# Causal mask added to the diagonal attention scores on TensorE, unmasked copies shared between ScalarE and VectorE

## The chip, the cores and the metric

The kernel runs on one core of a Trainium2 chip. The metric is the device time of one execution in microseconds (us), the median of the runs; less is better. Five engines work side by side, each through its own queue in order: TensorE (PE, with its weight loads shown apart as PEld), VectorE (DVE), ScalarE (ACT), GpSimd (POOL) and SyncE (SP), which issues most DMAs.

## The reference, cut to what matters

The program is one layer of a hybrid decoder for a prompt of 2048 tokens and for a small sample group. The change touches one of its four branches, the stick-breaking attention of the prompt: 8 heads of 64, strictly causal.

```python
def sb_block(q, k, v, bias, q_pos, k_pos):
    z = (jnp.einsum('nqhd,nkhd->nhqk', q, k).astype(jnp.float32) * (SB_HEAD_DIM ** -0.5)
         + bias.astype(jnp.float32)[None, :, None, None])
    mask = (k_pos[None, :] < q_pos[:, None])[None, None]
    log_beta = jax.nn.log_sigmoid(z)
    log_1m = jnp.where(mask, jax.nn.log_sigmoid(-z), 0.0)
    rc = lax.cumsum(log_1m, axis=3, reverse=True)
    a = jnp.exp(jnp.where(mask, log_beta + rc - log_1m, -jnp.inf))
    return jnp.einsum('nqhk,nkhd->nqhd', a.astype(v.dtype), v)
```

The kernel works without logarithms: with beta = sigmoid(z) and gamma = sigmoid(-z), the weight of key k is beta(k) times the product of gamma over all later visible keys. A key at or after its query must count as beta 0 and gamma 1.

## The kernel before, in words

The program has three stages that follow each other on TensorE: the input projections, with the sample group's attention over its cache beside them (to about 1476 us); the prompt's stick-breaking attention (`sb_prompt`, to about 1950 us), with bits of side work; and the output projection.

The attention runs over 4 head pairs (`hp`), and in each over 4 blocks of 512 queries (`qb`). A block goes through its chunks of 512 keys (`kc`) from the diagonal one (`kc == qb`, called `dg`) down to 0: 16 diagonal steps and 24 others. A step has 4 score pairs (two heads `hh`, times two pairs of 128-query tiles, `q2` = 0 and 2) and 8 turned tiles (4 rows `r` of 128 keys, times two heads):

- `score`: TensorE forms S (line L1267, two matmuls `x` for each of two query tiles `j`); ScalarE turns S into gamma (`gam`, L1271) and beta (`be`, L1272); VectorE runs the product from the right as a scan (`E`, L1337 on the diagonal, L1340 elsewhere); GpSimd multiplies beta by it (L1349). On the diagonal the width w is 256 for `q2` = 0 and 512 for `q2` = 2.
- `turn`: six score steps later TensorE transposes the weights of 128 keys into a PSUM tile `AT` (L1360; two buffers), and a copy takes them to SBUF as `at` (four buffers). On the diagonal the copy is VectorE's and multiplies by the triangle `tri`, which drops keys that are not before the query (L1364); elsewhere it is ScalarE's plain copy (L1366).
- `values`: two steps later again TensorE adds `at` times V into `av` (L1376). At the end of a block VectorE multiplies `av` by the gate (`sbo`, L1381), and `av` has one buffer.

The scan of a diagonal tile multiplies by unmasked gammas and takes the maximum with `ZM`, a PSUM tile that holds 1 from the query's own key on, so that the product starts anew there.

The order on TensorE is the order in which the code is written. On the other engines a scheduler orders the instructions when the program is built. The first two score pairs (`sb_early`, tile `Se`) are formed during the projections. Side work on the output weights, the convolution branch and the end of the sample group is let in by costs that `sb_prompt` yields with each step.

Of the kernel before, what the change touches and what calls it, by code (L numbers as in the profile page):

```python
# [8 lines left out]
F32 = mybir.dt.float32  # L9
F32R = mybir.dt.float32r  # L10
# [3 lines left out]
ALU = mybir.AluOpType  # L14
# [4 lines left out]
P = 128  # L19
# [43 lines left out]
KT = 2  # L63
WR = 2


# [22 lines left out]
def kernel(  # L89
# [69 lines left out]
    ident = con.tile([P, P], F32, name="ident")  # L159
# [1077 lines left out]
    def sb_loader(sbr):  # L1237

        KT, V = {}, {}

        def load(hp, qb):
# [19 lines left out]

        return load, values

    def sb_scores(S, h, q2, w, Q, kt):
        for j in range(2):
            for x in range(2):
                pe.matmul(S[:, j, :w], lhsT=Q[:, x, P * (q2 + j) : P * (q2 + j + 1)], rhs=kt[:, :w], start=x == 0,  # L1267
                          stop=x == 1)

    def sb_gates(S, h, w, ga, be):  # L1270
        act.activation(out=ga, in_=S[:, :, :w], func=AF.Sigmoid, bias=nbias_bc[:, h : h + 1], scale=-1.0)  # L1271
        act.activation(out=be, in_=S[:, :, :w], func=AF.Sigmoid, bias=bias_bc[:, h : h + 1])  # L1272

    def sb_early(load, blk, sbr, bps, early):

        room = sbr.tile([P, 16, P], F32, tag="V", name="early", bufs=2).rearrange("p (n j b) c -> p n j (b c)", n=4, j=2)
        for n in range(2):
            blk[0, n] = load(0, n)
        for _ in range(3):
            yield  # L1280
        for hh in range(2):
            S = bps.tile([P, 512], F32, tag="AT", name=f"Se{hh}", bufs=2).rearrange("p (j k) -> p j k", j=2)
            Q, KT, _ = blk[0, 0]
            sb_scores(S, hh, 0, 2 * P, Q[hh], KT[0, hh, 0])
# [4 lines left out]
    def sb_prompt(load, loaded, sb, bps, ops, zmp, early, values_of, flags, newest):  # L1289

# [63 lines left out]
        def turn(hp, qb, kc, r, hh):  # L1354
# [7 lines left out]
            c = slice(P * q0, 512)  # L1362
            if dg:
                dve.tensor_tensor(out=at[:, c], in0=ap_[:, c], in1=tri[:, : 512 - P * q0], op=ALU.mult)  # L1364
            else:
                act.copy(at[:, c], ap_[:, c])  # L1366
            ats[hp, qb, kc, r, hh] = at
# [513 lines left out]
    S = {}  # L1881
# [23 lines left out]
    for cost in main():  # L1905
        tasks.step()
        due += rate * cost
        while sample is not None and due >= 1.0:
            due -= 1.0
            try:  # L1910
# [5 lines left out]
                sbr = bx.enter_context(tc.tile_pool(name="sbr", bufs=1, side="right", reuse_waits="tile"))  # L1916
                load, values_of = sb_loader(sbr)
                bps = bx.enter_context(tc.tile_pool(name="bps", bufs=1, space=PSUM, side="right", reuse_waits="tile"))
                starts = sb_early(load, blk, sbr, bps, early)
                next(starts)  # L1920
# [86 lines left out]
    due, steps = 0.0, 0  # L2007
    for cost in sb_prompt(load, blk, sb, bps, ops, zmp, early, values_of, flags, newest):
        steps += 1
# [164 lines left out]
```

## Time and profile before

| | |
|---|---|
| runs of the kernel before | 2357.12, 2351.18, 2350.86 us; median 2351.18 |
| profiled execution, first to last instruction | 2357.7 us |
| mean granted TensorE clock | 0.994 |
| PE busy over the whole span | 2270.5 us, 96% |
| window 1485 to 1950 us (attention) | PE 441.1, DVE 391.0, ACT 400.1, POOL 371.1 of 465 us |

The page and the answers give busy times by engine and line, idle times with what ended them, and the order in time. A busy PE is not a PE at its peak, since the ends of its pipelined matmuls are modelled: what one matmul costs its successors is the distance between starts, not its length. For the profiled execution the span is the only time known; it lies 6.5 us over the median of the runs.

### The profile page before, as it was taken

The page shows a single profiled execution, that of the slowest core. Times are in us where ns is not written, and L with a number is a line of the kernel's source. Part 1 is how long each engine was busy: PE and PEld are TensorE (multiplying, and loading weights), DVE is VectorE, ACT ScalarE, POOL GpSimd, SP SyncE. Part 2 cuts the span into 40 slices and gives each one's busy share as a digit, 9 for nine tenths or more (in the row PEclk, how much of TensorE's full clock was granted, in tenths as well). Part 3 has the DMA queues.
Part 4 walks back from the last instruction along what each step waited for, and adds up shares of the span by engine and source line. Part 5 has one row for each costly group of instructions (what it writes and reads, how often), then busy time and mean ns, then how long its engine had stood idle before and what let it go on. Part 6 is the DMA issues. An engine that isn't in the chain of part 4 may idle for free. (4 is left out here: it accounts for less than half of the span.)

```text
span 2357.7 us, 42145 instructions
## 1 busy us (share of the span) xinstructions
PE 2270.5 (96%) x16000; PEld 1762.9 (75%) x16000; DVE 1705.4 (72%) x2372; ACT 1115.4 (47%) x1935; POOL 1299.0 (55%) x1347
## 2 busy tenths in 40 slices
PE   7999999999999999999999999899999999999997
PEld 7898888888888777777777777555555557788775
DVE  5342786969657673577787868988897966586997
ACT  5332342242442322224242324798989875453553
POOL 3554546555565546545546463688988854432333
PEclk9999999999999999999999999999999999999999
DMA  6689987878678899987877785656544207876764
GB/s 208 199 293 308 332 273 255 278 254 290 240 260 314 314 350 341 321 286 257 304 264 258 274 269 148 178 166 167 163 124 117 77 23 231 277 230 190 244 244 145
DMA packets 336868, 557.94 MB, mean 237 GB/s; under 512 B 27985, under 2 KB 212433, under 8 KB 320266
## 3 DMA queue, kind: packets, MB, share of 16 engines
q1 hardware_dynamic: 281290, 286.53, 39.3%
q0 software_dynamic: 55376, 268.72, 32.0%
q8 instruction: 126, 2.06, 0.3%
q14 instruction: 76, 0.62, 0.1%
HBM read 465.09 MB, written 90.68 MB: 236 GB/s over the span
## 5 line engine op out<-in xcount | busy, mean ns | idle before, releaser
L971 DVE STREAM_TRANSPOSE T<-kt 128x1024 f32<-128x1024 f32 x256 | 308.7, 1226 | 188.7 <-PE sSA L984 176.3
L938 POOL DMA_INDIRECT vt<-in_cache_v_dram,idv x256 | 253.2, 989 | 256.1 <-PE sO L1023 195.3
L623 DVE SCALAR_TENSOR_TENSOR cacc<-U,par,cacc 128x512 f32<-128x512 f32 x480 | 359.9, 750 | 11.0
L1349 POOL TENSOR_TENSOR be<-be,E 128x512 f32<-128x512 f32 (+3 forms) x316 | 300.3, 965 | 59.6 <-DVE E L1340 26.7
L1340 DVE TENSOR_TENSOR_SCAN E<-gam,cr,ZM 128x513 f32<-128x513 f32 x192 | 232.8, 1263 | 14.2 <-ACT gam L1271 10.8
L938 POOL DMA_INDIRECT kt<-in_cache_k_dram,idk x128 | 127.7, 998 | 196.4 <-DVE T L971 151.3
L1360 PEld LDWEIGHTS AT<-ident,be 128*128 128x128 f32 x1082 | 115.7, 141 | 130.0 <-ACT at L1366 48.3
L1993 PE MATMUL acc<-wohi,mh 128*128 128x512 f32 (+1 forms) x480 | 194.2, 405 | 1.2 <-ACT mh L1717 1.2
L1271 ACT ACTIVATE gam<-S,nbias_bc 128x1024 f32<-128x1024 f32 (+1 forms) x158 | 173.1, 1096 | 42.4 <-ACT be L1272 19.4
L1993 PE MATMUL acc<-wolo,mh 128*128 128x512 f32 (+1 forms) x480 | 190.4, 397 | 0.7 <-DVE wolo L1628 0.7
L1993 PE MATMUL acc<-wohi,ml 128*128 128x512 f32 x448 | 178.6, 399 | 8.0 <-DVE ml L1728 8.0
L1267 PE MATMUL S<-kT,Q 128*128 128x512 f32 (+1 forms) x632 | 173.6, 397 | 4.3 <-ACT be L1272 4.3
L1272 ACT ACTIVATE be<-S,bias_bc 128x1024 f32<-128x1024 f32 (+1 forms) x158 | 172.1, 1089 | 0.8 <-DMA gsd<-sg1sg 0.8
L1360 PE MATMUL AT<-ident,be 128*128 128x128 f32 x1082 | 157.0, 282 | 15.7 <-DVE at L1364 8.6
L1376 PE MATMUL av<-at,V 128*64 128x512 f32 (+3 forms) x640 | 151.9, 554 | 3.5 <-DVE sbo L1381 3.5
L984 PE MATMUL sSA<-T,W 128*32 128x128 f32 x4096 | 140.0, 276 | 2.8 <-DVE T L971 1.4
L984 PEld LDWEIGHTS sSA<-T,W 128*32 128x32 f32 x4096 | 105.3, 109 | 38.7 <-issue 31.9
L1728 DVE TENSOR_TENSOR ml<-mr,mh 128x512 fp32r<-128x512 f32 x108 | 93.2, 869 | 45.2 <-ACT mh L1717 43.5
L1023 PE MATMUL sO<-vt,saT 128*32 128x512 f32 x1024 | 122.4, 592 | 0.0
L1267 PEld LDWEIGHTS S<-kT,Q 128*128 128x128 f32 x632 | 104.3, 192 | 18.1 <-ACT be L1272 5.8
L1366 ACT COPY at<-AT 128x512 f32<-128x512 f32 x192 | 111.3, 680 | 12.2 <-PE AT L1360 12.2
L1337 DVE TENSOR_TENSOR_SCAN E<-gam,ZM 128x384 f32<-128x384 f32 (+1 forms) x124 | 94.3, 811 | 28.8 <-ACT gam L1271 21.9
(584 smaller groups left out, 6021.5 us busy)
## 6 DMA issues: line engine op xcount, KB each, us to landing
Q<-qd SPq DMA_DIRECT2D x64, 256.0 KB
mr<-mixd SPq DMA_DIRECT2D x32, 512.0 KB
mr<-mixd SPq DMA_DIRECT2D x48, 256.0 KB
xtp<-in_x_prompt_dram SPq DMA_DIRECT2D x16, 512.0 KB
kT<-kd SPq DMA_DIRECT2D x64, 128.0 KB
ws<-in_w_out_dram SPq DMA_DIRECT2D x16, 512.0 KB
wsd<-ws SPq DMA_DIRECT2D x16, 512.0 KB
msd<-mr SPq DMA_DIRECT2D x32, 256.0 KB
```

The lines of the kernel that those rows point to most:

```text
L623: dve.scalar_tensor_tensor(out=ps, in0=U[:, a + k : a + k + H], scalar=wd[:, k : k + 1], in1=ps, op0=ALU.mult, op1=ALU.add)
L938: pool.indirect_dma_start(out=dst, out_offset=None, in_=rows, in_offset=bass.IndirectOffsetOnAxis(ap=idx, axis=0))
L971: S["turn"] = dve.transpose(T[:, 2 * hh : 2 * hh + 2].rearrange("p s j t -> p (s j t)"), kt[:, 2 * hh : 2 * hh + 2].rearrange("p s j d -> ...
L984: pe.matmul(sSs[n][32 * g : 32 * g + 32, P * ml : P * (ml + 1)], lhsT=W[:, jj, :], rhs=T[:, :, jj, :], start=i == 0, stop=i == 3, tile_pos ...
L1267: pe.matmul(S[:, j, :w], lhsT=Q[:, x, P * (q2 + j) : P * (q2 + j + 1)], rhs=kt[:, :w], start=x == 0, stop=x == 1)
L1271: act.activation(out=ga, in_=S[:, :, :w], func=AF.Sigmoid, bias=nbias_bc[:, h : h + 1], scale=-1.0)
L1272: act.activation(out=be, in_=S[:, :, :w], func=AF.Sigmoid, bias=bias_bc[:, h : h + 1])
L1340: dve.tensor_tensor_scan(out=E[:, j][:, ::-1], data0=g_[:, j][:, ::-1], data1=ZM[:, 0:1].to_broadcast([P, 513]), initial=carry[hh, q2][:, ...
L1349: newest.append(pool.tensor_tensor(out=be[:, j, :m], in0=be[:, j, :m], in1=E[:, j, 513 - w : 513 - w + m], op=ALU.mult).ins)
L1360: pe.transpose(ap_[:, P * qt : P * (qt + 1)], A[hp, qb, kc, hh, qt][:, P * r : P * (r + 1)], ident)
L1376: pe.matmul(av[64 * hh : 64 * hh + 64, c], lhsT=V[:, 4 * kc + r, 64 * hh : 64 * hh + 64], rhs=ats.pop((hp, qb, kc, r, hh))[:, c], start=dg ...
L1993: pe.matmul(o[:rows], lhsT=m[a][:, k, :rows], rhs=W[prod, 4 * h + k][w], start=not cont and h == k == n == 0, stop=h == 1 and k == 3 and n ...
```

## The change

A constant tile `later` is made once in `sb_loader`: its first half is the identity in float32r, its second half a 128x128 triangle `shut` that is 0 where the key comes before the query and -1e30 elsewhere. In each diagonal score, `sb_scores` adds a third matmul per query tile between the two it has: identity times triangle, into the 128 columns that lie on the diagonal. After the gates such a key has beta 0 and gamma 1. The triangle `tri` and its multiplication go; all 320 turned tiles are plain copies. Which engine copies is decided as the program is built: a running account (`spent`) of the attention's own work on ScalarE and VectorE, with one linear cost for the gates, the scans and each engine's copy, and a rule that no account lags the other by more than `SLACK` = 3 us.

```diff
+SHUT = -1e30
+SLACK = 3.0
...
     def sb_loader(sbr):
...
+        later = sbr.tile([P, 2, P], F32R, name="later", bufs=1)
+        shut = sbr.tile([P, P], F32, name="shut", bufs=1)
+        pool.memset(shut, 0.0)
+        pool.affine_select(out=shut, in_=shut, compare_op=ALU.is_gt, fill=SHUT, base=0, pattern=[[-1, P]],
+                           channel_multiplier=1)
+        pool.tensor_copy(later[:, 0], ident)
+        pool.tensor_copy(later[:, 1], shut)
...
-    def sb_scores(S, h, q2, w, Q, kt):
+    def sb_scores(S, h, q2, w, Q, kt, later=None):
         for j in range(2):
+            n = P * (q2 + j + 1)
             for x in range(2):
                 pe.matmul(S[:, j, :w], lhsT=Q[:, x, P * (q2 + j) : P * (q2 + j + 1)], rhs=kt[:, :w], start=x == 0,
                           stop=x == 1)
+                if later is not None and x == 0:
+                    pe.matmul(S[:, j, n - P : n], lhsT=later[:, 0], rhs=later[:, 1], start=False, stop=False)
...
-        tri = sb.tile([P, 512], F32, name="tri", bufs=1)
-        pool.memset(tri, 1.0)
-        pool.affine_select(out=tri, in_=tri, compare_op=ALU.is_gt, fill=0.0, base=0, pattern=[[1, 512]],
-                           channel_multiplier=-1)
...
+        spent = {act: 0.0, dve: 0.0}
+
+        def spend(eng, us):
+            spent[eng] += us
+            other = dve if eng is act else act
+            spent[other] = max(spent[other], spent[eng] - SLACK)
...
-                sb_scores(S, h, q2, w, Q[hh], KT[hp, hh, kc])
+                sb_scores(S, h, q2, w, Q[hh], KT[hp, hh, kc], later if dg else None)
+                spend(act, 2 * (0.15 + 0.00166 * w))
...
                 E = sb.tile([P, 2, 513], F32, tag="E", name=f"E{nm}", bufs=3)
+                spend(dve, 0.3 + 0.00204 * sum(ns))
...
-            if dg:
-                dve.tensor_tensor(out=at[:, c], in0=ap_[:, c], in1=tri[:, : 512 - P * q0], op=ALU.mult)
+            n = 512 - P * q0
+            mine, its = 0.045 + 0.00083 * n, 0.13 + 0.00104 * n
+            if spent[act] + mine <= spent[dve] + its:
+                act.copy(at[:, c], ap_[:, c])
+                spend(act, mine)
             else:
-                act.copy(at[:, c], ap_[:, c])
+                dve.tensor_copy(at[:, c], ap_[:, c])
+                spend(dve, its)
```

TensorE keeps its order, with 128 matmuls put in. Its queue at the first score pair of a diagonal step (the digits in a tile's name are the block, chunk and so on; the last number is a tile's own) read before:

```order
L1267 MATMUL S_3_3_0_0_15592<-kT_3_0_15177,Q_3_0_15178 128x256 x4
L1376 MATMUL av_2_15453<-at_2_1_0_0_15534,V_14881 64x512
L1376 MATMUL av_2_15453<-at_2_1_0_1_15541,V_14881 64x512
L1360 MATMUL AT_2_1_2_0_15607<-ident,be_2_1_0_0_15307 128x128 x2
L1360 MATMUL AT_2_1_2_0_15607<-ident,be_2_1_0_2_15338 128x128 x2
```

and reads now:

```order
L1277 MATMUL S_3_3_0_0_15621<-kT_3_0_15198,Q_3_0_15199 128x256
L1280 MATMUL S_3_3_0_0_15621<-later 128x128
L1277 MATMUL S_3_3_0_0_15621<-kT_3_0_15198,Q_3_0_15199 128x256 x2
L1280 MATMUL S_3_3_0_0_15621<-later 128x128
L1277 MATMUL S_3_3_0_0_15621<-kT_3_0_15198,Q_3_0_15199 128x256
L1396 MATMUL av_2_15482<-at_2_1_0_0_15563,V_14890 64x512
```

Nothing else moved on TensorE; each of the 128 mask matmuls stands between two matmuls with other weights. VectorE's queue where the first head pair's last diagonal tiles are copied (scans are printed as SCALAR_TENSOR_TENSOR) read before:

```order
L1340 SCALAR_TENSOR_TENSOR E_3_2_0_2_15816<-gam_14875,cr_3_3_0_2_15693,ZM 128x513 x2
L1364 TENSOR_TENSOR at_3_3_0_0_15799<-AT_3_3_0_0_15794,tri 128x512
L1364 TENSOR_TENSOR at_3_3_0_1_15806<-AT_3_3_0_1_15801,tri 128x512
L1340 SCALAR_TENSOR_TENSOR E_3_2_1_0_15849<-gam_14877,cr_3_3_1_0_15724,ZM 128x513 x2
L1381 TENSOR_TENSOR sbo_2_15826<-av_2_15453,sgt_2_15189 128x512
L1364 TENSOR_TENSOR at_3_3_1_0_15833<-AT_3_3_1_0_15829,tri 128x384
L1364 TENSOR_TENSOR at_3_3_1_1_15839<-AT_3_3_1_1_15835,tri 128x384
L1340 SCALAR_TENSOR_TENSOR E_3_2_1_2_15879<-gam_14879,cr_3_3_1_2_15756,ZM 128x513
L1364 TENSOR_TENSOR at_3_3_2_0_15862<-AT_3_3_2_0_15859,tri 128x256
L1364 TENSOR_TENSOR at_3_3_2_1_15867<-AT_3_3_2_1_15864,tri 128x256
```

and reads now:

```order
L1356 SCALAR_TENSOR_TENSOR E_3_2_0_2_15853<-gam_14884,cr_3_3_0_2_15730,ZM 128x513
L1385 COPY at_2_0_3_0_15804<-AT_2_0_3_0_15799 128x512
L1356 SCALAR_TENSOR_TENSOR E_3_2_0_2_15853<-gam_14884,cr_3_3_0_2_15730,ZM 128x513
L1356 SCALAR_TENSOR_TENSOR E_3_2_1_0_15886<-gam_14886,cr_3_3_1_0_15761,ZM 128x513 x2
L1385 COPY at_3_3_0_1_15843<-AT_3_3_0_1_15838 128x512
L1401 TENSOR_TENSOR sbo_2_15863<-av_2_15482,sgt_2_15210 128x512
L1356 SCALAR_TENSOR_TENSOR E_3_2_1_2_15916<-gam_14888,cr_3_3_1_2_15793,ZM 128x513 x2
L1356 SCALAR_TENSOR_TENSOR E_3_1_0_0_15941<-gam_14884,cr_3_2_0_0_15825,ZM 128x513 x2
L1356 SCALAR_TENSOR_TENSOR E_3_1_0_2_15976<-gam_14886,cr_3_2_0_2_15856,ZM 128x513 x2
```

Seven of the eight diagonal copies have left VectorE here, and a copy of the chunk before (`at_2_0_3_0`), which was ScalarE's, stands between two scans. The other seven are now on ScalarE, between its gates (`gam`, `be`):

```order
L1382 COPY at_3_3_0_0_15836<-AT_3_3_0_0_15831 128x512
L1283 ACTIVATE gam_14888<-S_3_2_1_2_15845,nbias_bc 128x2x512
L1284 ACTIVATE be_3_2_1_2_15850<-S_3_2_1_2_15845,bias_bc 128x1024
L1382 COPY at_3_3_1_0_15870<-AT_3_3_1_0_15866 128x384
L1382 COPY at_3_3_1_1_15876<-AT_3_3_1_1_15872 128x384
L1283 ACTIVATE gam_14884<-S_3_1_0_0_15878,nbias_bc 128x2x512
L1284 ACTIVATE be_3_1_0_0_15883<-S_3_1_0_0_15878,bias_bc 128x1024
```

Before, ScalarE had only gates there. Over the whole attention the copies fall so:

| copies of `at`, by width | 512 | 384 | 256 | 128 |
|---|---|---|---|---|
| before: VectorE, diagonal | 32 | 32 | 32 | 32 |
| before: ScalarE, elsewhere | 192 | | | |
| now: VectorE, diagonal | 12 | 8 | 8 | 4 |
| now: VectorE, elsewhere | 54 | | | |
| now: ScalarE, diagonal | 20 | 24 | 24 | 28 |
| now: ScalarE, elsewhere | 138 | | | |

More of the change, by code (lines that the diff above doesn't have):

```diff
@@ L1260, in values @@
             sp.dma_start(V[hp], vd[:, P * hp : P * (hp + 1)].rearrange("(t p) c -> p t c", p=P))
-        return load, values
-    def sb_scores(S, h, q2, w, Q, kt):
+        return load, values, later
+    def sb_scores(S, h, q2, w, Q, kt, later=None):
         for j in range(2):
+            n = P * (q2 + j + 1)
             for x in range(2):
@@ L1272, in sb_gates, with sb_early @@
         act.activation(out=be, in_=S[:, :, :w], func=AF.Sigmoid, bias=bias_bc[:, h : h + 1])
-    def sb_early(load, blk, sbr, bps, early):
+    def sb_early(load, blk, sbr, bps, early, later):
         room = sbr.tile([P, 16, P], F32, tag="V", name="early", bufs=2).rearrange("p (n j b) c -> p n j (b c)", n=4, j=2)
@@ L1283, in sb_early @@
             Q, KT, _ = blk[0, 0]
-            sb_scores(S, hh, 0, 2 * P, Q[hh], KT[0, hh, 0])
+            sb_scores(S, hh, 0, 2 * P, Q[hh], KT[0, hh, 0], later)
             early[hh] = room[:, 2 * hh], room[:, 2 * hh + 1]
@@ L1287, in sb_early, with sb_prompt @@
             yield
-    def sb_prompt(load, loaded, sb, bps, ops, zmp, early, values_of, flags, newest):
+    def sb_prompt(load, loaded, sb, bps, ops, zmp, early, values_of, flags, newest, later):
         zm = sb.tile([P, 512], F32, tag="sbo", name="zm", bufs=1)
@@ L1916 @@
                 sbr = bx.enter_context(tc.tile_pool(name="sbr", bufs=1, side="right", reuse_waits="tile"))
-                load, values_of = sb_loader(sbr)
+                load, values_of, later = sb_loader(sbr)
                 bps = bx.enter_context(tc.tile_pool(name="bps", bufs=1, space=PSUM, side="right", reuse_waits="tile"))
-                starts = sb_early(load, blk, sbr, bps, early)
+                starts = sb_early(load, blk, sbr, bps, early, later)
                 next(starts)
@@ L2007 @@
     due, steps = 0.0, 0
-    for cost in sb_prompt(load, blk, sb, bps, ops, zmp, early, values_of, flags, newest):
+    for cost in sb_prompt(load, blk, sb, bps, ops, zmp, early, values_of, flags, newest, later):
         steps += 1
```

## Prediction

> **What bounds the kernel now.** I read the share of busy time, then the windows of the attention, then what TensorE waited for there.
>
> ```profile
> PE 2270.5 (96%) x16000; PEld 1762.9 (75%) x16000; DVE 1705.4 (72%) x2372; ACT 1115.4 (47%) x1935; POOL 1299.0 (55%) x1347
> ...
> 1485.00:1950.00 465.00, 441.10 (x2450) 258.40 (x2449) 391.01 (x485) 400.11 (x527) 371.09 (x469) 1.00 0.44 123
> 1500.00:1515.00 15.00, 10.92 (x63) 6.63 (x64) 15.00 (x23) 9.11 (x12) 8.57 (x11) 1.00 0.49 111
> 1617.00:1628.00 11.00, 8.86 (x53) 5.01 (x51) 11.00 (x18) 7.48 (x10) 9.18 (x10) 1.00 0.67 206
> 1630.00:1642.00 12.00, 12.00 (x69) 6.95 (x66) 10.41 (x11) 11.88 (x16) 11.11 (x16) 1.00 0.12 40
> 1838.00:1848.00 10.00, 8.02 (x49) 4.47 (x47) 10.00 (x16) 6.59 (x8) 6.27 (x7) 1.00 0.60 180
> ```
>
> The columns of a window are its length and the busy time of PE, PEld, DVE, ACT and POOL. Over the attention TensorE is busy 441.1 of 465 us, so 23.9 us idle. Two kinds of stretch differ. Away from the diagonal (1630 to 1642) TensorE has no idle time and ScalarE hardly any. Where the short blocks of a head pair bring diagonal steps close together (1617 to 1628, 1838 to 1848, and 1500 to 1515 at the start) VectorE is the one that is always busy, and TensorE idles 2.1, 2.0 and 4.1 us. What ended its idle time in 1485 to 1950 (us in total, times, longest):
>
> ```profile
> PE AT L1360 <- DVE at L1364: 8.6, 11, 1.2
> PE AT L1360 <- ACT at L1366: 4.3, 12, 0.9
> PE av L1376 <- DVE sbo L1381: 3.5, 8, 1.9
> PE cm L1452 <- ACT at L1366: 1.7, 1, 1.7
> PE nS L1076 <- DVE at L1364: 1.6, 1, 1.6
> PE nys L1133 <- DVE at L1364: 1.4, 1, 1.4
> ```
>
> VectorE's masked copies (L1364) stand behind 8.6 + 1.6 + 1.4 = 11.6 us, ScalarE's copies (L1366) behind 4.3 + 1.7 = 6.0, the gate product behind 3.5. In the off-diagonal stretch the beat is TensorE's own:
>
> ```profile
> 1575.56 1.17 PE L1267 MATMUL S<-kT,Q 128*128 128x512 f32 x4
> 1576.66 1.08 PE L1376 MATMUL av<-at,V 128*64 128x512 f32 x4
> 1577.67 1.09 PE L1360 MATMUL AT<-ident,be 128*128 128x128 f32 x8
> 1578.52 1.17 PE L1267 MATMUL S<-kT,Q 128*128 128x512 f32 x4
> ...
> 1576.75 1.11 ACT L1366 COPY at<-AT 128x512 f32<-128x512 f32 x2
> 1577.69 1.19 ACT L1271 ACTIVATE gam<-S,nbias_bc 128x1024 f32<-128x1024 f32 x1
> 1578.70 1.19 ACT L1272 ACTIVATE be<-S,bias_bc 128x1024 f32<-128x1024 f32 x1
> 1579.70 1.15 ACT L1366 COPY at<-AT 128x512 f32<-128x512 f32 x2
> ```
>
> From one score pair to the next it is 2.96 us, without idle time between the groups, and ScalarE's round of two copies and two gates takes 1579.70 - 1576.75 = 2.95. So TensorE sets the pace with ScalarE right behind it, and VectorE sets it in the dense diagonal stretches. The attention ends in the output projection on the same TensorE queue, so what TensorE gains or loses here moves the end by as much.
>
> **The mask matmuls.** 64 diagonal score pairs with two query tiles each make 128 of them (4 in `Se`, in a stage where TensorE is busy anyway). No 128-column float32r matmul stands in the trace. The nearest rows are the same type at 256 columns, each with weights of its own, and a plain float32 product of 128 columns, in which each of four calls is two instructions:
>
> ```profile
> 1970.12 0.28 PE L1504 MATMUL cz<-shi,pwhi 128*128 128x256 f32 x1
> 1970.23 0.28 PE L1504 MATMUL cz<-slo,pwhi 128*128 128x256 f32 x1
> 1970.35 0.28 PE L1504 MATMUL cz<-shi,pwlo 128*128 128x256 f32 x1
> ...
> 136.06 1.05 PE L901 MATMUL qps<-qsT,rep 128*128 128x128 f32 x8
> ```
>
> At 256 columns starts lie 0.11 to 0.12 us apart. The eight instructions of L901 start (1.05 - 0.275) / 7 = 0.11 apart (0.275 is the length of one), so a whole float32 product costs 0.22. The transposes of L1360, 128 columns with new weights each time, also keep about 0.11: (1.09 - 0.27) / 7 = 0.117, over a beat with one longer step. I take 0.119, the upper edge of these, since the next weights must still be loaded while only 128 columns stream, and every full-array row with new weights stays at 0.11 or more: 128 x 0.119 = **+15.2 us**. Bounds: 0.06 if half the columns cost half (7.7 us), 0.22 if so narrow a float32r product runs at the float32 rate (28.2 us).
>
> [...]
>
> At the start of the attention some of it is free, because TensorE waits for the gates there:
>
> ```profile
> 1481.79 1.22 PE L1267 MATMUL S<-kT,Q 128*128 128x256 f32 x4 [3.03 <-ACT be L1272]
> 1484.32 3.30 PE L1267 MATMUL S<-kT,Q 128*128 128x512 f32 x8 [1.31 <-ACT be L1272]
> ```
>
> The 12 masks of the first two diagonal steps after `Se` lie at or beside these 4.3 us: 12 x 0.119 = **-1.4 us**.
>
> **The copies.** Durations (us busy, mean ns of one) by width:
>
> ```profile
> L1364 DVE TENSOR_TENSOR at<-AT,tri 128x512 f32<-128x512 f32 x32 | 20.5, 681 | 5.6 <-PE AT L1360 5.0
> L1364 DVE TENSOR_TENSOR at<-AT,tri 128x384 f32<-128x384 f32 x32 | 16.2, 546 | 0.0
> L1364 DVE TENSOR_TENSOR at<-AT,tri 128x256 f32<-128x256 f32 x32 | 11.7, 406 | 0.0
> L1364 DVE TENSOR_TENSOR at<-AT,tri 128x128 f32<-128x128 f32 x32 | 7.6, 273 | 0.0
> L1340 DVE TENSOR_TENSOR_SCAN E<-gam,cr,ZM 128x513 f32<-128x513 f32 x192 | 232.8, 1263 | 14.2 <-ACT gam L1271 10.8 <-POOL be L1349 2.7 <-POOL ws L1587 0.7
> L1366 ACT COPY at<-AT 128x512 f32<-128x512 f32 x192 | 111.3, 680 | 12.2 <-PE AT L1360 12.2
> ```
>
> Before, VectorE spends 20.5 + 16.2 + 11.7 + 7.6 = 56.0 us on copies. A plain copy out of PSUM I price as the masked one (it streams the same elements; L443, a 256-wide plain copy, is in the next fence with 420 ns against 406): 66 x 0.681 + 8 x 0.546 + 8 x 0.406 + 4 x 0.273 = 53.7. So VectorE's total hardly falls; the work only moves from diagonal to other steps. ScalarE's goes from 111.3 to 158 x 0.58 (111.3 / 192) for the wide ones plus the narrow ones by these rows:
>
> ```profile
> L382 ACT COPY nat0v<-nt0v 128x384 f32<-128x384 f32 x8 | 3.8, 481 | 18.6 <-PE nt0v L375 18.6
> L1013 ACT COPY saT<-sSA 128x256 f32<-128x256 f32 x64 | 23.9, 374 | 47.5 <-PE sSA L1011 47.5
> L443 DVE COPY mnat<-mt 128x256 f32<-128x256 f32 x8 | 3.4, 420 | 15.5 <-PE mt L441 15.5
> ```
>
> 24 x 0.481 + 24 x 0.374 + 28 x 0.27 (the step of 0.107 taken once more) = 28.1, so 119.7: +8.4 us, in diagonal steps.
>
> What that buys is the waits. A dense diagonal stretch has about two diagonal steps, 2 x 3.5 = 7.0 us of masked copies (56.0 / 16 a step). In the new order the second head pair's stretch holds four copies of 512, two of 384, two of 256 and one of 128 on VectorE: 4.9 us, 2.1 less. TensorE gets 16 x 0.119 = 1.9 us more to do there. VectorE was 2.1 us too slow, so it is no longer last. The first block, with the sample group's small VectorE work between, I leave 2 of its 4.1 us: of 11.6 us **-9.6**. ScalarE loses 54 of its 192 wide off-diagonal copies, 54 x 0.58 / 24 = 1.3 us of a step of 4 x 2.96, so most of its 6.0 us goes, the one at `cm` in the last stretch less surely: **-3.5**. The 3.5 us behind `sbo` stay: `av` has one buffer, and the product follows the last `av` at once.
>
> The new wait: 54 off-diagonal copies now stand in VectorE's queue behind scans of 1.26 us. There VectorE had 2 x 1.26 = 2.5 of a beat of 2.96 in scans; with 54 / 96 of a copy per beat it has 2.9. Queued behind such a copy are the next scan, GpSimd's product and the transposes six steps on; TensorE waits for it if `AT` is not free when its turn comes a beat later. At the earliest 0 us; at most a third of the 54 are late by what a late VectorE copy costs now, 11.6 / 13 = 0.9 us, 16 us. I take **+2.0**, near the lower end, since a scan and a copy (1.95 us) fit into a beat.
>
> **Small parts at nothing.** The four GpSimd instructions that make `later` stand after the probabilities' scaling, ahead of the sample group's `nM`; its neighbours end near 1456.7 and the first reader comes at 1470.26:
>
> ```profile
> 1456.44 0.26 POOL L1087 TENSOR_SCALAR_AFFINE_SELECT nM<-nM 32x32 f32<-32x32 f32 x1
> 1470.26 0.64 PE L1267 MATMUL Se<-kT,Q 128*128 128x256 f32 x4
> ```
>
> Four like it are about 1 us and 13 us of cover; without that, 1 us. Making `tri` no longer delays the start of the scans, by at most as much. SP's loads keep their lines with a few neighbours swapped, each far ahead of its use.
>
> **The sum.** +15.2 - 1.4 - 9.6 - 3.5 + 2.0 = +2.7 us. The profiled execution would take 2357.7 + 2.7 = 2360.4; against the median 2351.2 it is **2353.9**, 0.1%: a draw. Under about 0.3% (7 us) a measurement of this kernel can't tell from no change, as its runs differ by 6 us.
>
> **Rivals.** *The waits go and the masks are cheap*: all 11.6 + 6.0 us behind copies vanish, no new ones come, and a mask costs 0.08, between 0.06 and 0.119: 128 x 0.08 - 1.4 - 17.6 = -8.8, so 2342. For it: the waits gather in few places, and the account levels just these. Against: no full-array row with new weights goes below 0.11. *Narrow float32r is slow*: a mask runs at the 0.22 of L901: +28.2 in place of +15.2, so +15.7, 2367, slower. It decides in TensorE's score groups; from about 0.155 us a mask the kernel is 7 us slower. For it: no 128-wide float32r row shows the contrary. Against: from 512 to 256 columns the price fell in step. *The waits only change their owner*: VectorE has 53.7 us of copies after 56.0, on steps where it had 0.45 us of a beat free; a third of the 54 late makes +16 in place of +2, so +16.7, 2368.
>
> **Chances.** The draw 0.47, its own range 2345 to 2360; the gain 0.2; slow narrow matmuls 0.2; new waits 0.13. The draw's upper edge lies past 2358, so: faster by over 0.3% (under 2344.1) 0.2, within 0.45, slower (over 2358.2) 0.35. Range for 8 in 10: 2342 to 2367, from the gain to the slow masks.
>
> **What would show it.** In the profile after, line L1280 has 128 matmuls, and starts in a diagonal score group tell their price: a group of two 256-wide pairs with masks should take 0.24 us longer than 0.72. TensorE's idle time behind VectorE's copies should fall from 11.6 to about 4 us in the dense diagonal stretches, with VectorE under 100% there, and ScalarE should show slack off the diagonal. I am wrong if a mask costs over 0.155 us, if waits for VectorE copies appear in off-diagonal steps, or if the time moves outside 1476 to 1950.

## The result, and the profile after

| | before | after |
|---|---|---|
| runs, median (us) | 2354.15 (2350.86 to 2358.86) | 2373.14 (2369.6 to 2382.94) |
| profiled execution, span (us) | 2357.7 | 2373.5 |
| copies `at` on VectorE / ScalarE | 128 / 192 | 86 / 234 |

After over before is 1.0081, with a 95% interval of 1.0059 to 1.0104: 19 us slower (14 to 24), where the forecast was 2.7 us and a draw. The profiled executions differ by 15.8 us.

The share of busy time and the windows of the attention after the change; a window's columns are its length and the busy time of PE, PEld, DVE, ACT and POOL, then PE's granted clock:

```profile
PE 2286.4 (96%) x16128; PEld 1781.8 (75%) x16128; DVE 1699.4 (72%) x2330; ACT 1125.0 (47%) x1977; POOL 1296.8 (55%) x1349
...
1485.00:1965.00 480.00, 455.57 (x2554) 273.79 (x2554) 387.45 (x443) 411.10 (x571) 370.87 (x468) 0.99 0.43 118
1500.00:1515.00 15.00, 11.54 (x65) 6.90 (x62) 12.48 (x19) 10.59 (x18) 8.32 (x12) 0.89 0.39 83
1617.00:1628.00 11.00, 8.88 (x52) 5.04 (x50) 10.94 (x13) 9.74 (x14) 11.00 (x11) 1.00 0.79 227
```

TensorE is busy 16 us longer, with 128 more instructions. The attention's window is drawn 15 us longer, and TensorE's idle time in it is as before: 480 - 455.6 = 24.4 against 23.9. In the dense diagonal stretch at 1617, which the new split was to relieve, VectorE is as full as it was (10.94 of 11), and TensorE idles 2.1 us as before. What TensorE waited for after the change (us in total, times, longest):

```profile
PE AT L1376 <- DVE at L1385: 15.1, 14, 3.1
PE AT L1376 <- ACT at L1382: 4.1, 5, 1.9
PE S L1277 <- ACT be L1284: 3.1, 2, 2.6
PE AT L1376 <- POOL be L1365: 1.0, 1, 1.0
PE nys L1135 <- ACT at L1382: 0.9, 1, 0.9
PE av L1396 <- DVE sbo L1401: 0.8, 1, 0.8
PE cm L1472 <- ACT at L1382: 0.6, 1, 0.6
PE nS L1078 <- DVE at L1385: 0.6, 1, 0.6
```

Behind VectorE's copies it waits 15.1 + 0.6 = 15.7 us, where it waited 11.6. Behind ScalarE's it is 5.6 for 6.0, behind the gate product 0.8 for 3.5.

To set these against the masks I cut each trace between the first matmul into `Se` and the start of the last `av`, and split that stretch of TensorE into idle time (from the end of one matmul to the start of the next), what windows at half clock cost (half of the busy time in them), and the rest, which is matmuls at their own pace. The half is an estimate: in after, at a granted clock of 0.50, a score group of four 512-wide matmuls with two masks takes 2.42 us to the start of the next group (1863.19 to 1865.61), and at 1.00 it takes 1.33 (1628.44 to 1629.77).

| us | length | idle | half clock | rest |
|---|---|---|---|---|
| before | 475.6 | 28.2 | 2.7 | 444.7 |
| after | 492.5 | 27.0 | 6.6 | 458.8 |

So +16.9 = +14.1 (rest) - 1.2 (idle) + 4.0 (half clock), more than the whole difference of the two executions. The masks cost what was forecast. What was to come back as idle time did not: in these terms the forecast was +15.2 for the masks and -12.5 of idle time (-1.4 - 9.6 - 3.5 + 2.0). Idle time fell by 1.2, which is 11.3 us short, and half clock, for which the forecast had no term, took 4.0. Behind the attention no kernel of this study changes anything, and yet the traced executions take between 401 and 412 us from the last `av` to their end (412 before), so traces are compared by this stretch, and whole times by the ratios. The same mask from the trace's side, by line:

```profile
L1280 PEld LDWEIGHTS S<-later x124: 187/192/338, 1478.6 to 1899.6; 128*128 128x128 f32 x124
L1280 PE MATMUL S<-later x124: 220/222/312, 1478.9 to 1899.8; 128*128 128x128 f32 x124
...
1657.45 0.37 PE L1277 MATMUL S<-kT,Q 128*128 128x256 f32 x1
1657.65 0.23 PE L1280 MATMUL S<-later 128*128 128x128 f32 x1
1657.71 0.45 PE L1277 MATMUL S<-kT,Q 128*128 128x256 f32 x2
1658.00 0.22 PE L1280 MATMUL S<-later 128*128 128x128 f32 x1
1658.06 0.33 PE L1277 MATMUL S<-kT,Q 128*128 128x256 f32 x1
```

The first two rows give min, median and max length in ns of the weight load and the matmul. A score group of two 256-wide pairs with its two masks lasts from 1657.45 to 1658.06 + 0.33 = 1658.39, that is 0.94 us for the 0.72 or 0.73 without masks: 0.11 for a mask.

### The profile page after: what moved, and what is told of

Same layout as the page of the kernel before. It is cut to its first block, busy times and chain, and to the rows that moved or that the text cites. A ratio compares the mean times of both kernels' runs of the same rounds, so it can differ in the third digit from the quotient of the medians.

```text
span 2373.5 us, 42401 instructions
## 1 busy us (share of the span) xinstructions
PE 2286.4 (96%) x16128; PEld 1781.8 (75%) x16128; DVE 1699.4 (72%) x2330; ACT 1125.0 (47%) x1977; POOL 1296.8 (55%) x1349
## 5 line engine op out<-in xcount | busy, mean ns | idle before, releaser
L1356 DVE TENSOR_TENSOR_SCAN E<-gam,cr,ZM 128x513 f32<-128x513 f32 x192 | 233.9, 1266 | 11.8 <-ACT gam L1283 10.0
L1277 PE MATMUL S<-kT,Q 128*128 128x512 f32 (+1 forms) x632 | 189.2, 410 | 3.1 <-ACT be L1284 3.1
L1283 ACT ACTIVATE gam<-S,nbias_bc 128x1024 f32<-128x1024 f32 (+1 forms) x158 | 167.6, 1061 | 33.0 <-PE S L1277 28.1
L1376 PE MATMUL AT<-ident,be 128*128 128x128 f32 x1082 | 160.3, 283 | 21.1 <-DVE at L1385 15.1
L1284 ACT ACTIVATE be<-S,bias_bc 128x1024 f32<-128x1024 f32 (+1 forms) x158 | 166.5, 1054 | 0.7 <-DMA gsd<-sg1sg 0.7
L1382 ACT COPY at<-AT 128x512 f32<-128x512 f32 (+3 forms) x234 | 117.8, 541 | 29.2 <-PE AT L1376 28.5
L1277 PEld LDWEIGHTS S<-kT,Q 128*128 128x128 f32 x632 | 109.1, 193 | 15.8 <-ACT be L1284 3.7
```

What stands on the lines that cost most here:

```text
L1356: dve.tensor_tensor_scan(out=E[:, j][:, ::-1], data0=g_[:, j][:, ::-1], data1=ZM[:, 0:1].to_broadcast([P, 513]), initial=carry[hh, q2][:, ...
L1376: pe.transpose(ap_[:, P * qt : P * (qt + 1)], A[hp, qb, kc, hh, qt][:, P * r : P * (r + 1)], ident)
```

## The experiments

A trace's instructions can be matched one by one with the program's, so I also measured how late a copy is: from the end of the last transpose of its tile to the copy's start (ns, mean and the value that 9 of 10 stay under).

| copies | before | after | e9_inorder |
|---|---|---|---|
| VectorE, diagonal | 990, 1845 | 1326, 2508 | 770, 1072 |
| VectorE, off-diagonal | none | 1089, 2744 | 130, 147 |
| ScalarE, off-diagonal | 868, 1473 | 526, 1125 | 575, 1418 |

ScalarE's off-diagonal copies came earlier, as the prediction wanted. VectorE's came later: one in ten starts over 2.5 us after its transposes, the time of two 1.26 us scans.

**Which part costs.** Two theories stood at first. T1: the masks make up the loss, and the split returns nothing. T2: most masks fit into old waits, and the split costs.

e1_masks, the masks alone:

```diff
-            if spent[act] + mine <= spent[dve] + its:
-                act.copy(at[:, c], ap_[:, c])
...
+            if dg:
+                dve.tensor_copy(at[:, c], ap_[:, c])
+            else:
+                act.copy(at[:, c], ap_[:, c])
```

> The mask matmuls alone: they stay as in the change, and every copy goes back to its old engine (VectorE on the diagonal, plain, ScalarE off it). T1 (a mask costs its 0.11 to 0.12 us of TensorE, 14 us in all, and the new split of the copies returns nothing, since its waits only change owner): +8 to +14 us over the kernel before, the part below 14 being masks that fit into the old waits behind VectorE in the dense diagonal stretches. T2 (most masks fit into those old waits, and the new split is what costs): at most +4. The prediction's own terms: 15.2 - 1.4 = +13.8 less what the 11.6 us of waits absorb.

Measured: ratio 1.0027 (1.0012 to 1.0042), +6 us. Idle 22.6, half clock 2.8, rest 457.7. Its waits:

```profile
PE AT L1376 <- DVE at L1382: 6.8, 10, 0.9
PE AT L1376 <- ACT at L1384: 3.6, 6, 1.0
...
PE av L1394 <- DVE sbo L1399: 2.1, 8, 0.5
```

The masks take 13.0 us (457.7 - 444.7), and 5.6 us of idle time goes. It goes a little at every kind of wait: 1.6 us behind VectorE's copies (10.0 are left: 6.8, and in rows not shown 1.8 at `nS` and 1.4 at `nys`), 1.4 behind the gate product, 1.3 behind the gates and 0.7 behind ScalarE's copies. That lies between T1 and T2.

e2_copies, the split alone (the two mask lines of `sb_scores` deleted):

> The new split of the copies alone: the mask matmuls are left out, so the diagonal scores stay unmasked and later keys enter the output. T1: the split returns nothing, -1 to +4 us against the kernel before, with about 15 us of TensorE's idle time still behind VectorE's copies. T2: the split itself costs, +10 to +16. The prediction's own terms, -9.6 - 3.5 + 2.0: -11 us.

Measured: 1.0066 (1.0052 to 1.0080), +16 us, T2's figure. Idle 34.8, half clock 4.6, rest 445.7. Its waits:

```profile
PE AT L1374 <- DVE at L1383: 18.4, 19, 2.4
PE AT L1374 <- ACT at L1380: 6.3, 13, 1.7
```

T1 falls: the split by itself is the larger half of the loss. The two parts add up within their intervals (0.27 + 0.66 = 0.93%, together 0.81%).

e3_double, each mask matmul issued twice:

```diff
                 if later is not None and x == 0:
                     pe.matmul(S[:, j, n - P : n], lhsT=later[:, 0], rhs=later[:, 1], start=False, stop=False)
+                    pe.matmul(S[:, j, n - P : n], lhsT=later[:, 0], rhs=later[:, 1], start=False, stop=False)
```

> The change with every mask matmul issued twice (what is shut stays shut). T1: 128 more at 0.11 to 0.12 us, +13 to +15 us over the change, since there the diagonal steps have no spare time on TensorE. T2: +4 at most. Slow narrow matmuls (0.155 us or more each): +20 or more.

Measured: 1.0126 (1.0112 to 1.0141), 11 us over the change by the ratios, a little under T1's range. In the trace the rest grows by 472.5 - 458.8 = 13.7 us, 0.107 a mask, as T1 had it, while idle time falls by 2.0.

e4_split, the kernel before with each masked copy cut in two:

```diff
             if dg:
-                dve.tensor_tensor(out=at[:, c], in0=ap_[:, c], in1=tri[:, : 512 - P * q0], op=ALU.mult)
+                d = slice(P * q0, P * q0 + P)
+                dve.tensor_tensor(out=at[:, d], in0=ap_[:, d], in1=tri[:, :P], op=ALU.mult)
+                if r < 3:
+                    act.copy(at[:, P * q0 + P :], ap_[:, P * q0 + P :])
```

> The kernel before, with each masked copy cut in two: VectorE multiplies only the 128 columns of the diagonal block by the triangle, ScalarE copies the columns behind them plainly; no mask matmul, off-diagonal copies on ScalarE. VectorE's copies fall from 56.0 to 128 x 0.273 = 35 us and leave the scans' queue sooner, ScalarE gains 32 x (0.481 + 0.374 + 0.27) = 36 us in diagonal steps. If the waits behind VectorE's copies in the dense stretches come from VectorE's load: -4 to -10 us. If they only change owner (ScalarE's two gates are ahead of the copy in its queue, as VectorE's scans were): -1 to +4.

Measured: 1.0002 (0.9990 to 1.0014). Waits behind VectorE's products fall to 2.5 us, and those behind ScalarE's copies rise from 6.0 to 14.6. The second reading held: they changed owner.

**Where the split costs.** By the matching, the 15 waits of after that end at a copy on VectorE (15.7 us) are seven at an off-diagonal one (6.6 us) and eight at a diagonal one (9.0 us, with the one of 3.1). (The expectation of e7 below counts eight and 7.7: it takes in a wait of 1.0 us that ended 0.08 us after an off-diagonal copy, together with the GpSimd product to which the profile puts it down.) One of them by time; first what VectorE did, then TensorE:

```profile
1658.11 2.46 DVE L1356 TENSOR_TENSOR_SCAN E<-gam,cr,ZM 128x513 f32<-128x513 f32 x2 [0.53 <-ACT gam L1283]
1660.48 0.67 DVE L1385 COPY at<-AT 128x512 f32<-128x512 f32 x1
1661.06 0.99 DVE L1353 TENSOR_TENSOR_SCAN E<-gam,ZM 128x128 f32<-128x128 f32 x2
...
1656.82 0.87 PE L1376 MATMUL AT<-ident,be 128*128 128x128 f32 x6
...
1659.53 0.66 PE L1376 MATMUL AT<-ident,be 128*128 128x128 f32 x4
1661.20 0.66 PE L1376 MATMUL AT<-ident,be 128*128 128x128 f32 x4 [1.01 <-DVE at L1385]
```

The transposes this copy needs end at 1656.82 + 0.87 = 1657.69, and it starts 2785 ns later. VectorE stood idle at that time, for 0.53 us, but in its queue two full scans come first, and the first of them waits for its gate. TensorE fills the other `AT` buffer at 1659.53 and then waits 1.01 us for this one. T3: the loss is copies behind pairs of full scans, above all the 54 off-diagonal ones.

e5_swap writes a step's transposes and copies ahead of the older scan pair, and e6_swapbefore does so in the kernel before:

```diff
-                        if len(pend) == 2:
-                            pend.pop(0)()
-                        pend.append(rest)
                         yield cost / 2
                         behind(step)
                         step += 1
+                        if len(pend) == 2:
+                            pend.pop(0)()
+                        pend.append(rest)
```

> The change, with the transposes and copies of a step written ahead of the older step's scan pair instead of behind it (TensorE's order of work is the same; the account then also splits a little otherwise). T3 (the split costs because a copy on VectorE stands behind a pair of full-width scans, 2 x 1.26 us): waits of TensorE behind VectorE's copies fall from 15.7 to 5 to 8 us, +8 to +12 over the kernel before. Rival (VectorE is simply too full, and whatever comes second is late): the scans are late instead and GpSimd's products with them, +15 to +20.

> The same swap in the kernel before (masked copies, no mask matmul): of the 11.6 us behind masked copies those of 1 us at the start of the dense diagonal stretches go. T3: -4 to -8. Rival (VectorE too full there): the scans late instead, 0 to +4.

Measured: 1.0086 (1.0058 to 1.0114), +20 us, and 1.0015 (0.9997 to 1.0032), +4 us. T3 missed in both, and the rival's figures came in both. In e5 its reason did not: the waits behind VectorE's copies rose to 22.1 us, four of them over 1.7 us, and none of TensorE's waits is put down to GpSimd's products. The place in the code does not set VectorE's order, since the scheduler does, and it put three scans ahead of some copies (two started 3.28 us after their transposes, behind three scans of 1.26). In e6 the rival's reason came too: the waits behind masked copies fell (8.6 to 4.9 at the transposes), those behind GpSimd's products rose from 0.7 to 6.9, and the time didn't fall.

e7_diagonly lets the account share the diagonal copies only:

```diff
-            if spent[act] + mine <= spent[dve] + its:
+            if not dg or spent[act] + mine <= spent[dve] + its:
```

> The change, but the account shares only the diagonal copies; all 192 off-diagonal copies go back to ScalarE. T3: the 8 waits of 1 us behind VectorE's off-diagonal copies go (7.7 us, with one half-clock window 9), ScalarE's come back to what they were before (about +3): +9 to +13 over the kernel before. Rival (any split of the copies is as bad, since the diagonal ones wait behind the same scans): +15 to +19. The prediction's accounting has no cost in the off-diagonal copies (+2.0 of its sum): as the change.

Measured: 1.0072 (1.0046 to 1.0098), +17 us, the rival's. One row of its waits, and two of VectorE's copies:

```profile
PE AT L1376 <- DVE at L1385: 17.4, 13, 3.1
...
L1385 DVE COPY at<-AT 128x512 f32<-128x512 f32 x19 | 12.6, 679 | 4.0 <-PE AT L1376 4.0
L1385 DVE COPY at<-AT 128x384 f32<-128x384 f32 x12 | 6.5, 538 | 0.1
```

T3's aim at the off-diagonal copies falls. Here VectorE has 43 copies and 23.1 us of them, less than half of before's 56.0, and TensorE waits more for them. The sum of VectorE's work isn't the cause. These 13 waits are at diagonal copies; the 11 of them over 1 us are behind two or three full scans.

e8_at3 gives the change a third PSUM buffer for the turned tiles, by moving the scans' operand `ZM` to SBUF:

```diff
-        ZM = zmp.tile([P, 512], F32, name="ZM", bufs=1)
+        ZM = sb.tile([P, 512], BF16, name="ZM", bufs=1)
...
+            if count["turn"] % 3:
+                ap_ = bps.tile([P, 512], F32, tag="AT", name=f"AT{nm}", bufs=2)
+            else:
+                ap_ = zmp.tile([P, 512], F32, tag="AT3", name=f"AT{nm}", bufs=1)
```

> The change, with a third PSUM buffer for the transposed weights (its bank is freed by moving the scans' second operand to SBUF, in bfloat16). T3: TensorE returns to a buffer one group later, and no copy is more than about 4 us late, so most of the 20 us of waits behind copies go: +2 to +7 over the kernel before, which leaves about the price of the masks and some idle time of the start. Rival (VectorE and ScalarE are short of time over the whole stage, so a buffer only delays the wait): +13 to +19. If the scans' operand in SBUF makes scans longer (1.27 us now), that is in the trace.

Measured: 1.0705 (1.0679 to 1.0730). The scans became longer (1974 ns for 1266), so the run says nothing on the buffer (see the last section). That question stays open.

**Order or time.** T4: the loss is the order of VectorE's queue. T5: VectorE has no time to spare, in whatever order. The next four runs put VectorE's queue in the order of the code during the attention:

```diff
+    held = ExitStack()
+    held.enter_context(tc.manual_schedule(engines={mybir.EngineType.PE, mybir.EngineType.DVE}))
     for cost in sb_prompt(load, blk, sb, bps, ops, zmp, early, values_of, flags, newest, later):
...
+    held.close()
```

e9_inorder is that in the change, e10_inorderswap with e5's edit too, e11_inorderbefore in the kernel before, e12_inordermasks in e1's kernel.

> The change, with VectorE's queue in the order in which the code is written during the attention (as TensorE's is), so that the scheduler can't put further scan pairs ahead of a copy. T4 (the split costs because of VectorE's queue order: in it 25 copies follow three or more full-width scans, where the kernel before had that only after long runs of steps without a copy): waits behind VectorE's copies fall from 15.7 to under 8 us, and half-clock windows that follow them go: +3 to +9 over the kernel before, of which the masks are most. T5 (VectorE is short of time, order does not matter): the waits stay or move to GpSimd's products and the gates, +15 or more.

> As the run with VectorE in written order, and each step's copies are written ahead of the older step's scan pair. T4: no copy stands behind its own step's pair any more: +1 to +8. T5: +15 or more. If the copies, waiting for their transposes at the head of VectorE's queue, hold up the scans: waits behind GpSimd's products appear, +10 to +20.

> The kernel before, with VectorE's queue in written order during the attention. T4: its four waits of 1.1 us at the ends of the dense diagonal stretches (a masked copy behind two full-width scans) stay or halve: -5 to +1. T5: 0 to +6.

> The mask matmuls alone (every copy on its old engine), with VectorE's queue in written order. T4: as the masks alone (+6) or up to 5 us less. T5: as the masks alone or up to 6 us more.

Measured: e9 1.0062 (1.0036 to 1.0087), e10 1.0387 (1.0345 to 1.0429), e11 1.0114 (1.0071 to 1.0158), e12 1.0158 (1.0119 to 1.0197). By its time (+15 us, 8 to 20) e9 is T5's, by its waits it is not. e11 (+27) and e12 (+37) lie beyond both their readings, and e10 (+91) is covered only by T5's "or more". e9's first waits, and VectorE at the start of the attention:

```profile
PE AT L1376 <- DVE at L1385: 15.1, 1, 15.1
PE AT L1376 <- POOL be L1365: 5.3, 9, 0.9
...
1497.11 0.43 DVE L1111 STREAM_TRANSPOSE nanT<-nbe 32x256 f32<-32x256 f32 x1
1510.96 0.49 DVE L1122 TENSOR_SCALAR nrb<-ident,ngc 128x128 f32<-128x128 f32 x2 [13.42 <-DMA ngc<-gnd]
```

Behind VectorE's copies there is one wait of 15.1 us, and beside it one of 0.3. In written order an instruction of the sample group that waits 13.42 us for a DMA stands ahead of that copy. The 54 off-diagonal copies now start 130 ns after their transposes (1089 before this edit). e11 and e12 have the same long wait (12.2 and 15.9 us), and in e11 a wait of 0.8 to 1.1 us stands at the end of nine of the 16 diagonal steps, where a masked copy follows a scan pair: with the old owners, written order is the worse one. e10 shows the sign that its expectation named last: 37.1 us of waits for GpSimd's products, which fits copies that wait at the head of VectorE's queue and hold up the scans. Its +91 us are far more than the 10 to 20 that this reading allowed.

The next three keep the scheduler for the first two blocks and use written order from the third on, so that the 15.1 us go:

```diff
             if bi == 0:
                 values_of(0)
+            if bi == 2:
+                held.enter_context(tc.manual_schedule(engines={mybir.EngineType.PE, mybir.EngineType.DVE}))
```

e13_later is the change with this, e14_latercopies that without the mask matmuls. e15_block has no mask matmul either, but a triangle on VectorE:

```diff
+            if dg:
+                d = slice(P * q0, P * q0 + P)
+                dve.tensor_tensor(out=at[:, d], in0=ap_[:, d], in1=later, op=ALU.mult)
+                spend(dve, 0.27)
+                c = slice(P * q0 + P, 512)
```

> The change, with VectorE's queue in written order from the third block of the attention on, so that the sample group's small work at the start, which held a copy back by 15.1 us when the whole stage was in written order, is left to the scheduler as before. T4 (VectorE's queue order is what the split costs): the 15.1 us become the 3 us of the change and the half-clock windows behind them go (17.1 us at half rate, of which 10 to 14 go): -3 to +5 over the kernel before, that is 14 to 21 us under the change. T5 (time, not order): +12 or more.

> The same without the mask matmuls (later keys of the diagonal block enter the output unmasked). T4: the split returns here what the prediction gave it and more, -8 to -16 against the kernel before, and the difference to the run with masks is their price, 11 to 15 us. T5: +0 or more.

> No mask matmul: VectorE multiplies only the 128 columns of the diagonal block by a triangle, the columns behind it and the off-diagonal copies are shared by the account, VectorE in written order from the third block on. VectorE has 128 x 0.273 = 35 us of products in diagonal steps beside its share of the copies. T4: -12 to -4 against the kernel before (no TensorE price, little waiting). If each diagonal product, written behind its step's scan pair, is late: waits of 0.8 us at some 12 to 24 places, 0 to +10.

Measured: e13 1.0011 (0.9994 to 1.0028), e14 0.9972 (0.9953 to 0.9992), e15 1.0004 (0.9987 to 1.0022). e13's waits, and VectorE's 512-wide copies in it:

```profile
PE AT L1376 <- POOL be L1365: 4.7, 8, 0.9
PE S L1277 <- ACT be L1284: 4.2, 3, 2.6
PE AT L1376 <- DVE at L1385: 3.5, 2, 3.1
PE AT L1376 <- ACT at L1382: 2.3, 6, 0.7
...
L1385 DVE COPY at<-AT 128x512 f32<-128x512 f32 x66 | 45.4, 689 | 57.4 <-PE AT L1376 56.7 <-ACT be L1284 0.5
```

| us | length | idle | half clock | rest |
|---|---|---|---|---|
| e2, split alone | 485.0 | 34.8 | 4.6 | 445.7 |
| e14, the same in written order | 472.4 | 23.7 | 5.7 | 443.0 |
| after | 492.5 | 27.0 | 6.6 | 458.8 |
| e13, the same in written order | 481.3 | 19.9 | 4.5 | 457.0 |

The same copies on the same engines by the same account cost +16 us in the scheduler's order and return 7 us (2 to 11) in written order, just short of T4's 8 to 16. Compared by operation, tile and width, ScalarE's order in the attention is nearly the same in e13 as in after (584 of 587 instructions match), and GpSimd's differs in about 25 of 490. VectorE is not short of time: in e13 it stands idle for 57.4 us ahead of its 512-wide copies (2.2 in after), and TensorE waits less for them. T5 falls and T4 stands: the split's loss is the order of VectorE's queue. With the masks the total is +3 us (-1 to +7), and the difference of e13 and e14, 9 us by the ratios and 14.0 in the rest column, is the masks' price. In e15 T4's -12 to -4 missed and the second reading held: it has no mask on TensorE, waits 5.2 us behind VectorE in 11 places and 5.1 behind ScalarE, and is a draw.

Is written order simply the better one? The traces, one execution each, answer this from the first score of the fourth block (of 16) to the last `av`, behind the sample group's long wait:

| us from the fourth block on: length, idle | scheduler's order | written order |
|---|---|---|
| old owners, no mask matmuls | 403.3, 15.1 (before) | 421.0, 23.4 (e11) |
| new owners, no mask matmuls | 412.4, 22.3 (e2) | 401.0, 13.3 (e14) |
| old owners, masks | 411.4, 12.8 (e1) | 425.9, 19.6 (e12) |
| new owners, masks | 421.5, 19.0 (after) | 408.0, 9.6 (e9) and 408.3, 9.8 (e13) |

It is not: with the old owners written order costs 14 to 18 us, with the new ones it returns 11 to 14. Order and owners have to fit each other. Behind its one long wait e9 is as quick as e13.

e16_bf16 makes the mask cheaper, if its type matters:

```diff
-        later = sbr.tile([P, 2, P], F32R, name="later", bufs=1)
+        later = sbr.tile([P, 2, P], BF16, name="later", bufs=1)
```

> As e13 (masks, shared copies, VectorE in written order from the third block on), with the two 128x128 matrices of the mask matmul in bfloat16 in place of float32r (0, 1 and -1e30 rounded; what is shut stays shut). A float32r mask costs 0.11 us of TensorE by the difference of e13 and e14 (14.5 us of its busy time over 128). If the price is that of loading and streaming 128 columns whatever the type: the same as e13, -1 to +6 over the kernel before. If it goes with the bytes of an operand: 0.06 each, 7 us less than e13, -8 to -1.

Measured: 1.0001 (0.9986 to 1.0016), the draw of the first reading. By the time alone the second isn't quite out (-3 to +4 us against its -8 to -1), but the rest is 458.3 us, no less than e13's 457.0. The weight load halves (a median of 95 ns for e13's 192) and the matmul doesn't get shorter (230 for 223):

```profile
L1280 PEld LDWEIGHTS <-later x128: 94/95/146, 1465.6 to 1883.7; 128*128 128x128 bf16 x128
L1280 PE MATMUL S<-later x124: 228/230/331, 1472.7 to 1883.7; 128*128 128x128 bf16 x124
```

No run that computes the whole reference beats the kernel before: e4, e13, e15 and e16 are draws with it.

## Why the prediction was wrong, step by step

**The masks (+15.2): right.** 14.1 us by after's rest column, 0.110 each; 13.0 in e1, 14.0 from e14 to e13. The score group grew by 0.21 to 0.22 us for the 0.24 forecast. The rival of slow narrow matmuls (0.22 each) is out. So is 0.08, the gain's price.

**Free masks at the start (-1.4): about right.** The gate waits there went from 4.3 to 3.1 us.

**What the copies take: right.** By width after the change:

```profile
L1385 DVE COPY at<-AT 128x512 f32<-128x512 f32 x66 | 44.2, 670 | 2.2 <-PE AT L1376 2.1
...
L1382 ACT COPY at<-AT 128x512 f32<-128x512 f32 x158 | 92.2, 617 | 24.1 <-PE AT L1376 23.6
L1382 ACT COPY at<-AT 128x384 f32<-128x384 f32 x24 | 11.0, 488 | 2.1 <-PE AT L1376 1.9
L1382 ACT COPY at<-AT 128x256 f32<-128x256 f32 x24 | 8.1, 384 | 3.0 <-PE AT L1376 2.9
L1382 ACT COPY at<-AT 128x128 f32<-128x128 f32 x28 | 6.5, 292 | 0.0
```

ScalarE's are 92.2 + 11.0 + 8.1 + 6.5 = 117.8 us for the 119.7 forecast. VectorE's 512-wide ones take 670 ns for 681.

**The waits that were to go (-9.6 and -3.5): the steps that failed.** The argument was one of load: a dense stretch loses 2.1 us of VectorE's work, "VectorE was 2.1 us too slow, so it is no longer last". VectorE did not get slack there. In the stretch at 1617 it is busy 10.94 of 11 us with eight full scans and four copies, where it had six full scans, three short ones and eight copies, and a copy stands behind three scans:

```profile
1618.47 3.62 DVE L1356 TENSOR_TENSOR_SCAN E<-gam,cr,ZM 128x513 f32<-128x513 f32 x3
1622.01 0.27 DVE L1385 COPY at<-AT 128x128 f32<-128x128 f32 x1
```

The waits behind its copies went from 11.6 up to 15.7 us. e7 shows that less copy work on VectorE (23.1 us for 56.0) doesn't bring fewer waits, and e9 and e13, with the same copies in another order, show what does: how many scans stand in the queue ahead of a copy that TensorE waits for. Of the 3.5 on ScalarE's side 0.4 came.

**The new wait (+2.0): its reason failed.** "a scan and a copy (1.95 us) fit into a beat" counts one scan ahead of a copy. In the trace it is two or three, 2.5 to 3.8 us, and 2744 ns is the lateness that one in ten off-diagonal copies exceeds. Off-diagonal copies stand behind 6.6 us of after's waits, over the 2.0 and within the bounds of 0 to 16, and diagonal copies in the new order behind 9.0.

**The gate product (3.5 stays): wrong, to the good.** It fell to 0.8.

**Not in the sum: half clock, +4.0.** The prediction has no such term and gives no reason for leaving it out. Two of after's longest waits are each followed by a window at half clock, 3.4 of the 4.0 (last section).

The rival "the waits only change their owner" gave +16.7 and 2368, nearest to the measured +15.8 between the traces. Its size came from the off-diagonal copies alone and from VectorE being too full. e7 contradicts the first part and e13 the second, so that its figure is near is luck. Of the marks the prediction set itself, masks under 0.155 us held. Waits at VectorE copies in off-diagonal steps appeared, which it had named as a sign of being wrong, and the waits in the dense diagonal stretches did not fall to 4 us.

That the scheduler puts scans ahead of a copy is seen in the traces. Why it does so when the copies of a pair of tiles have two owners isn't shown.

## What to carry to other kernels

When work moves between engines, adding up busy time per beat isn't enough: look at what stands ahead of the moved instruction in the new engine's in-order queue, count the longest run of it, and compare that with how long the waiting engine can go on (what a further buffer would do is open, e8). Where a scheduler sets that order, moving work also reorders what did not move, so an undo of half the edit (e7) or a fixed order (e13) tells more than the edit's own arithmetic. Try the fixed order with the old owners too (e11): no order was the better one for both. And what is added to the engine that sets the pace is partly paid out of its waits: 13 us of masks alone cost 6 (3 to 10).

## What the hardware showed that was not expected

**Long waits were often followed by half clock.** After's two longest waits of TensorE between 1500 and 1950 us and the stretches that follow (clock in the third column from the end):

```profile
1503.66:1506.74 3.08, 0.00 (x0) 0.03 (x1) 3.08 (x6) 1.76 (x3) 2.20 (x3) 1.00 0.03 0
1507.75:1511.16 3.41, 3.41 (x11) 1.55 (x11) 3.27 (x5) 1.86 (x5) 3.12 (x3) 0.50 0.75 171
1860.22:1862.15 1.93, 0.00 (x1) 0.03 (x1) 0.87 (x1) 0.93 (x4) 1.79 (x3) 1.00 0.78 296
1862.74:1866.15 3.41, 3.41 (x15) 2.43 (x13) 1.00 (x2) 2.52 (x6) 3.20 (x5) 0.50 0.26 79
```

Each idle stretch of 3.08 and 1.93 us is followed by 3.41 us at half clock, which costs an estimated 1.7 more (half of it). In 16 traces of this study (all but e8 and e10), from 1485 us to 30 us before the last matmul, a window at half clock starts during, or at most 1.5 us after, 30 of 39 idle stretches over 2.2 us, 23 of 43 between 1.7 and 2.2, and 11 of 173 between 0.8 and 1.7. By these numbers a wait of 2 us costs an estimated 2 + 23/43 x 1.7 = 2.9 us on average.

**With the scan's second operand in SBUF, in bfloat16, two engines were slower.** e8 moved `ZM` there from PSUM, where it was float32. VectorE's scan and GpSimd's product and carry copy in e8, then the latter two after the change:

```profile
L1356 DVE TENSOR_TENSOR_SCAN E<-gam,cr,ZM 128x513 f32<-128x513 f32 x192 | 369.4, 1974 | 10.2 <-POOL be L1365 10.0 <-ACT gam L1283 0.2
...
L1365 POOL TENSOR_TENSOR be<-be,E 128x512 f32<-128x512 f32 (+3 forms) x316 | 434.8, 1396 | 7.2 <-DVE E L1353 2.6 <-DVE E L1356 2.4 <-ACT gam L1283 1.3
L1361 POOL COPY cr<-E 128x2 f32<-128x2 f32 x96 | 85.7, 892 | 0.0
```

```profile
L1365 POOL TENSOR_TENSOR be<-be,E 128x512 f32<-128x512 f32 (+3 forms) x316 | 300.3, 962 | 76.1 <-DVE E L1353 41.3 <-DVE E L1356 17.8 <-ACT at L1382 11.1
L1361 POOL COPY cr<-E 128x2 f32<-128x2 f32 x96 | 17.9, 186 | 9.0 <-DVE E L1356 4.4 <-DVE E L1353 2.0
```

The scan went from 1266 to 1974 ns, the product from 962 to 1396, the small copy from 186 to 892. The edit changed both place and type, and the run doesn't part them. GpSimd's instructions were not edited, and became slower all the same; what slowed them is not shown.

**A mask's price did not follow its bytes.** With half the bytes the weight load fell from 192 to 95 ns (e16), and TensorE's rest column stayed the same (458.3 for 457.0).
